# Mixing stage: homes of operands and order of the bonus changed; first stage: one norm chain for both token tiles

## The chip, the cores and the metric

The kernel runs on one core of one Trainium2 chip. The metric is device time in microseconds, as the median of several runs. Before the change it is 1272.42 us (three runs: 1272.36, 1272.42 and 1277.24).

## The reference

A decoder trunk of two layers on 256 tokens of width 1024, in float32. Each layer is

```python
x = x + 0.5 * swiglu_ffn(rms_norm(x, ffn1_norm_g[l]), ffn1_w_in[l], ffn1_w_out[l])
proj = rms_norm(x, mix_norm_g[l]) @ w_mix_in[l]
y_rwkv = rwkv7_time_mix(p_rwkv, ...)        # 8 heads of 64, state updated per token
y_moba = moba_attention(q_m, k_m, v_m, rel_bias)   # 8 heads, one causal block of 256
x = x + concat([y_rwkv, y_moba]) @ w_mix_out[l]
x = x + memory_cross_attention(rms_norm(x, xattn_norm_g[l]), rms_norm(mem, mem_norm_g[l]), w_q, w_kv, w_o)
x = x + 0.5 * swiglu_ffn(rms_norm(x, ffn2_norm_g[l]), ffn2_w_in[l], ffn2_w_out[l])
```

with a last RMS norm behind both layers. Within the time mix, `r`, `k` and `v` are columns of the projection, the state decays per token, and to its output comes the bonus `sum(r * k * r_k) * v` per head, before the gate g. The memory has 256 tokens, too; cross attention has 4 heads of 256.

## The kernel before, in words

*Precision and weights.* Every product runs as three TensorE matmuls: each operand is split into a rounded part `hi` and a remainder `lo`, and hi·hi, hi·lo and lo·hi are summed in PSUM (`mm3`). Weights arrive as 1 MB tiles `raw` that SyncE loads one after the other; two `raw` buffers exist, so a load is issued when the tile two before it has been split. A tile is split in two halves (or four quarters): ScalarE copies it to `whi`, VectorE subtracts to get `wlo` (`split`). Activations are split the same way: `xt` tiles hold hi and lo; ScalarE writes hi (copy, line 85), VectorE lo (lines 79 or 82).

*Stages.* A layer is: first feed-forward, mixing, cross attention, second feed-forward. In mixing (`rwkv`, `moba` and the generator `others`, which the stage's main loop interleaves) the time mix is computed in four chunks of 64 tokens, two chunks (`cp`) together. G is the accumulated decay and Gi its inverse; BK holds the chunk's b and k times Gi, ZL holds kk·G and r·G; their products are masked into XB and ZL, a triangular system is inverted (`both`, then M and W, assembled by VectorE from TensorE's transposes), and a sequential pass over the chunks gives y. The bonus lives in BV, which is the buffer of `km`: it is formed from r, k and r_k before r is multiplied by G, then multiplied by v, then gated. Between these steps TensorE works on the mixing's own projections (`in_w_mixa`), on the memory's K and V projections for cross attention (`in_w_k`, `in_w_v`, whose operand is `xt` from `memT`), and on MoBA's heads.

*Order.* Each engine runs its own list of instructions in a fixed order, which a scheduler makes from the order of the source and from hints (`after`, `marks`). Engines wait for one another through semaphores. A tile comes from a pool with a tag and a number of buffers (tag "e" 15 buffers, "xn" 4, each of the four tiles of an operand taking one); an operand in a tag can be written only when the former user of its buffer is done.

*Norms.* `norm_rows` sums squares of a token tile (ScalarE), adds them to v, and `rsqrt` finds the factor by an integer guess and Newton steps, seven small VectorE instructions on one column. In the first stage (`start`) this is done for two token tiles, one after the other; `spread` turns the two factors into a row rT, and two scaled copies `r` per tile serve ScalarE (`h`, line 352). Mixing's and cross attention's inputs are normed in `norm_T` (`xs`, line 208), transposed by TensorE (line 216) and split by `normed` into `xt`.

*Homes before.* The input operand xT of every stage has tag "xn", as has the memory's operand. For cross attention, K's transposed projection kT is evicted in mixing and split into an operand with tag "e" in `xattn`, under a hint that puts it into the MoBA stretch; so is Q's.

## Time and profile before

| what | value |
|---|---|
| median of three runs | 1272.42 us |
| profiled execution, time and span | 1276.54 us, 1274.5 us |
| granted TensorE clock | 0.998 of full speed |
| TensorE busy | 1255.0 us (98%), 8912 matmuls |
| TensorE weight loads busy | 1086.7 us (85%) |
| VectorE busy | 911.8 us (72%), 1713 instructions |
| ScalarE busy | 740.5 us (58%), 1385 instructions |
| DMA | 222.30 MB, mean 174 GB/s |

TensorE runs almost without a gap. In layer 0 mixing takes about 191 to 372 us of the span, cross attention until about 448, and layer 1 repeats layer 0 some 631 us later. A row of the timeline gives start, duration, engine, line, operation, output and inputs, shape and how many were merged; in brackets stands how long the engine idled ahead of it and who released it.

### The profile page before, as it was taken

To read this page: it belongs to the slowest core of one execution; us is meant where nothing else is said; L and a number is where in the kernel's file an instruction comes from. 1 tells how busy PE (TensorE), PEld (TensorE's weight loads), DVE (VectorE), ACT (ScalarE), POOL (GpSimd) and SP (SyncE) were. 2 spreads that over 40 slices of the span, in tenths; PEclk is the share of its full clock that TensorE was granted. 3 is DMA by queue.
4 is the path that set the end of the run, shared out by engine and by line. 5 is a ranking of instruction groups with operands and counts; after the bars stand their busy time and mean duration, and the time that the engine had idled before them with its cause. 6 is when DMAs were issued, how large, how long until landed. Compare 5 with 4: busy or idle time off the path is not lost.

```text
span 1274.5 us, 22364 instructions
## 1 busy us (share of the span) xinstructions
PE 1255.0 (98%) x8912; PEld 1086.7 (85%) x8912; DVE 911.8 (72%) x1713; ACT 740.5 (58%) x1385; POOL 50.0 (4%) x74
## 2 busy tenths in 40 slices
PE   9999999999999999999999999999999999999997
PEld 7888888998878888888888888899988798888886
DVE  7978557888787676665576665569888767766644
ACT  6755437675645565554365554467756545655543
POOL 0025000010000000000000000000100000000000
PEclk9999999999999999999999999999999999999999
DMA  8767653345244435555545546443441344445542
GB/s 296 262 227 264 223 220 133 131 145 174 85 165 167 158 133 176 195 186 211 198 146 185 198 173 232 174 164 135 166 151 39 132 178 165 166 175 188 196 171 96
DMA packets 36120, 222.30 MB, mean 174 GB/s; under 512 B 4616, under 2 KB 8240, under 8 KB 10800
## 3 DMA queue, kind: packets, MB, share of 16 engines
q1 hardware_dynamic: 33504, 213.06, 46.9%
q0 software_dynamic: 1936, 7.35, 1.8%
q8 instruction: 70, 1.15, 0.4%
q10 hardware_dynamic: 576, 0.46, 0.1%
q14 instruction: 34, 0.28, 0.1%
HBM read 218.75 MB, written 3.68 MB: 175 GB/s over the span
## 4 chain that ended last, share of the span: by engine, by line
PE 82%; DVE 9%; ACT 5%; DMA 2%; issue 2%; ACTq 0%; DVEq 0%; SPq 0%
PE acc L100 75%; PE pm L100 4%; DVE wlo L79 2%; ACT whi L85 1%; DMA raw<-in_w_q_dram 1%; PE tr L216 1%; PE tr L100 1%; DMA raw<-in_w_k_dram 1%; DVE km L82 1%; ACT e L451 0%; DVE wb L79 0%; DVE kk L79 0%; DVE BK L79 0%; DVE rt L82 0%; ACT UD L85 0%
## 5 line engine op out<-in xcount | busy, mean ns | idle before, releaser
L100 PE MATMUL acc<-xt,whi 128*128 128x512 f32 (+1 forms) x2496 | 679.9, 344 | 0.2
L79 DVE TENSOR_TENSOR wlo<-raw,whi 128x1024 fp32r<-128x1024 f32 (+1 forms) x450 | 461.1, 1040 | 237.8 <-ACT whi L85 236.6
L85 ACT ACTIVATE whi<-raw 128x1024 fp32r<-128x1024 f32 (+1 forms) x450 | 399.5, 910 | 338.0 <-PE acc L100 248.6
L100 PE MATMUL acc<-xt,wlo 128*128 128x256 f32 x1888 | 531.6, 282 | 0.8 <-DVE wlo L79 0.8
L100 PEld LDWEIGHTS acc<-xt,whi 128*128 128x128 f32 x2496 | 432.0, 190 | 64.2 <-issue 2.0
L100 PEld LDWEIGHTS acc<-xt,wlo 128*128 128x128 f32 x1888 | 358.8, 190 | 1.8 <-DVE wlo L79 1.1
L100 PE MATMUL acc<-whi,hT 128*128 128x512 f32 x704 | 218.5, 390 | 0.0
L100 PEld LDWEIGHTS acc<-whi,hT 128*128 128x128 f32 x704 | 132.2, 188 | 27.4
L100 PE MATMUL acc<-wlo,hT 128*128 128x512 f32 x352 | 137.2, 390 | 0.0
L100 PEld LDWEIGHTS acc<-wlo,hT 128*128 128x128 f32 x352 | 66.1, 188 | 13.8 <-DVE wlo L79 0.4
L79 DVE TENSOR_TENSOR z<-acc,z 128x256 f32<-128x256 f32 x160 | 66.9, 418 | 0.6 <-ACT z L85 0.3
L100 PE MATMUL acc<-wb,xt 128*128 128x512 f32 x240 | 62.6, 400 | 0.0
L85 ACT ACTIVATE z<-acc 128x256 f32<-128x256 f32 x160 | 58.7, 367 | 3.5 <-PE acc L100 3.3
L85 ACT ACTIVATE xt<-tr,par 128x128 fp32r<-128x128 f32 x112 | 37.8, 365 | 28.1 <-PE tr L216 17.7
L100 PEld LDWEIGHTS acc<-wb,xt 128*128 128x128 f32 x240 | 42.9, 188 | 9.9 <-ACT xt L85 1.9
L186 ACT ACTIVATE junk<-x 128x512 f32<-128x512 f32 x36 | 22.6, 629 | 44.6 <-DVE x L82 24.3
L82 DVE SCALAR_TENSOR_TENSOR xt<-tr,par,xt 128x128 fp32r<-128x128 f32 x112 | 35.9, 346 | 8.1 <-ACT xt L85 7.5
L100 PE MATMUL acc<-whi,oT 128*128 128x512 f32 x128 | 40.3, 394 | 0.0
L79 DVE TENSOR_TENSOR z<-z,z 128x256 f32<-128x256 f32 x80 | 34.0, 425 | 7.2
L85 ACT ACTIVATE hT<-z 128x256 fp32r<-128x256 f32 x80 | 32.0, 400 | 10.5 <-DVE z L79 10.5
L79 DVE TENSOR_TENSOR hT<-z,hT 128x256 fp32r<-128x256 f32 x80 | 33.5, 419 | 3.1 <-ACT hT L85 3.1
L373 ACT ACTIVATE z<-z 128x256 f32<-128x256 f32 x80 | 32.7, 409 | 0.3 <-DVE z L79 0.3
(271 smaller groups left out, 1189.7 us busy)
## 6 DMA issues: line engine op xcount, KB each, us to landing
raw<-in_w_f2i_dram SPq DMA_DIRECT2D x44, 1024.0 KB, 4.7
raw<-in_w_f1i_dram SPq DMA_DIRECT2D x42, 1024.0 KB, 4.8
raw<-in_w_f1o_dram SPq DMA_DIRECT2D x22, 1024.0 KB, 4.8
raw<-in_w_mixa_dram SPq DMA_DIRECT2D x22, 1024.0 KB, 4.8
raw<-in_w_f2o_dram SPq DMA_DIRECT2D x22, 1024.0 KB, 4.8
raw<-in_w_v_dram SPq DMA_DIRECT2D x8, 1024.0 KB, 4.8
raw<-in_w_k_dram SPq DMA_DIRECT2D x8, 1024.0 KB, 4.8
raw<-in_w_mixo_dram SPq DMA_DIRECT2D x8, 1024.0 KB, 4.9
```

The lines of the kernel that those rows point to most:

```text
L79: return V.tensor_tensor(out=out_, in0=a, in1=b, op=op)
L82: V.scalar_tensor_tensor(out_, a, s, b, op0=op0, op1=op1)
L85: return A.activation(out_, in_, AF.Copy, **k)
L100: return nc.tensor.matmul(o, a, b, start=start, stop=stop, skip_group_check=True).ins
L186: marks["square"] = A.activation(junk, xt[:, n * 512:(n + 1) * 512], AF.Square, scale=1.0 / 32.0, accum_out=ss[:, n:n + 1]).ins
L216: nc.tensor.transpose(p[:, k, :], xs[:, k * 128:(k + 1) * 128], ident)
L373: A.activation(sums[0], sums[0], AF.Silu)
```

## The change

Four edits. (1) `norm_rows` takes several token tiles and computes their factors as columns of one chain; the first stage and the memory's norm use it. (2) In mixing, r·G is written straight into ZL by VectorE; before, VectorE multiplied r by G in place and ScalarE copied it to ZL. The bonus's first step (km, from r) moves behind it. (3) The bonus's product with v moves behind the mark "half", which stands after the two additions to M. (4) Homes: cross attention's input xT moves from tag "xn" to "e", Q's operand from "e" to "xn"; the buffers for K's operand are taken at the end of mixing.

```diff
@@ -179,22 +179,28 @@
         V.tensor_scalar(aux[:, :, 8:12], par[:, :, P_LNG:P_LNG + 4], RS, None, op0=OP.mult)
 
 
-    def norm_rows(xt):
+    def square_sums(xt):
         ss = SM([128, 2], name="ss", tag="n2")
         for n in range(2):
             junk = SM([128, 512], name="junk", tag="k2")
             marks["square"] = A.activation(junk, xt[:, n * 512:(n + 1) * 512], AF.Square, scale=1.0 / 32.0,
                                            accum_out=ss[:, n:n + 1]).ins
-        v = SM([128, 1], name="v", tag="n1")
-        V.tensor_scalar(v, ss[:, 0:1], ss[:, 1:2], NORM_EPS, op0=OP.add, op1=OP.add)
-        return rsqrt(v, 1, "n1")
+        return ss
+
+    def norm_rows(*xs):
+
+        n = len(xs)
+        v = SM([128, n], name="v", tag="n1" if n == 1 else "n2")
+        for i, ss in enumerate([square_sums(z) for z in xs]):
+            V.tensor_scalar(v[:, i:i + 1], ss[:, 0:1], ss[:, 1:2], NORM_EPS, op0=OP.add, op1=OP.add)
+        return rsqrt(v, n, "n1" if n == 1 else "n2")
 
     def spread(rs):
 
         p = BANK("tr")
-        for t, r in enumerate(rs):
+        for t in range(2):
             rb = SM([128, 128], name="rb", tag="k1")
-            V.tensor_scalar(rb, r.to_broadcast([128, 128]), RS, None, op0=OP.mult)
+            V.tensor_scalar(rb, rs[:, t:t + 1].to_broadcast([128, 128]), RS, None, op0=OP.mult)
             nc.tensor.transpose(p[:, t * 128:(t + 1) * 128], rb, ident)
         rT = H([128, S], name="rT", tag="mo")
         copy(rT, p[:, 0:S])
@@ -231,14 +237,14 @@
     def put_pair(xT, j, src):
         split(xT[j][:, :, 0, :], xT[j][:, :, 1, :], src)
 
-    def normed(g):
+    def normed(g, tag):
 
         xT = []
 
         def do(t, later=False):
 
             if not xT:
-                xT.extend(XT())
+                xT.extend(XT(tag))
 
             def put(n, p):
                 for k in range(4):
@@ -396,7 +402,7 @@
                 elif i < 16:
                     nc.sync.dma_start(mems[n][:, j % 4, :], I["memt"][:, j, :])
             if i == 8:
-                rs = [norm_rows(z) for z in rows]
+                rs = norm_rows(*rows)
             elif i == 10:
                 rT = spread(rs)
             elif i > 10:
@@ -428,11 +434,11 @@
     def xattn(l, xT, kTf, vx, post, following):
 
         v, vgen = vx
-        kT = XT("e")
+        kTf, kT = kTf
         for j in range(4):
             with after([marks["chunk", 1]]):
                 put_pair(kT, j, kTf[j // 2][:, 2 * (j % 2):2 * (j % 2) + 2, :])
-        qT = XT("e")
+        qT = XT()
         oT = [None] * 4
         P_ = {}
 
@@ -700,19 +706,18 @@
         for cp in range(2):
             tt(BK[cp][:, :, :, 0:64], pv(a, cp), pv(Gi, cp), OP.mult)
             tt(BK[cp][:, :, :, 64:128], pv(km, cp), pv(Gi, cp), OP.mult)
-        BV = km
-        for p in range(4):
-            stt(BV[:, p, :], r[:, p, :], P(P_RK, p), km[:, p, :], OP.mult, OP.mult)
         ZL = [[None, None] for _ in range(2)]
         for cp in range(2):
             two = lambda z: ch(z)[:, :, 2 * cp:2 * cp + 2, :]
             tt(two(kk)[:, :, :, 1:64], two(kk)[:, :, :, 1:64], two(G)[:, :, :, 0:63], OP.mult)
-            tt(two(r), two(r), two(G), OP.mult)
             for e in range(2):
                 hs = half(e)
                 ZL[e][cp] = H([128, 2, 4, 128], name="ZL")
                 copy(ZL[e][cp][hs, :, :, uc(e)], pv(kk, cp)[hs])
-                copy(ZL[e][cp][hs, :, :, dc(e)], pv(r, cp)[hs])
+                tt(ZL[e][cp][hs, :, :, dc(e)], pv(r, cp)[hs], pv(G, cp)[hs], OP.mult)
+        BV = km
+        for p in range(4):
+            stt(BV[:, p, :], r[:, p, :], P(P_RK, p), km[:, p, :], OP.mult, OP.mult)
         shifted(6, v[:, 2:4])
         yield XA
         yield XBB
@@ -871,10 +876,11 @@
         spread_heads(bh, ph, C_TM)
         yield first
         values(1)
-        for n, z in enumerate(of_heads(bh, C_HT, "acc")):
-            tt(ch(BV)[:, :, n, :], z, ch(v)[:, :, n, :], OP.mult)
+        bonus = of_heads(bh, C_HT, "acc")
         yield next(levels)
         with after([marks["half"]]):
+            for n, z in enumerate(bonus):
+                tt(ch(BV)[:, :, n, :], z, ch(v)[:, :, n, :], OP.mult)
             for p in range(4):
                 stt(BV[:, p, :], BV[:, p, :], P(P_LNB, p), g[:, p, :], OP.add, OP.mult)
         yield from levels
@@ -1049,12 +1055,13 @@
                 while due > 0:
                     due -= next(fill, 1e9)
         run(fill)
+        kx = XT("e")
         run(og)
-        return kT, (v, lambda: run(v_block(mT, 1)))
+        return (kT, kx), (v, lambda: run(v_block(mT, 1)))
 
 
     norms = [(l, g) for l in range(L) for g in (G_FFN1, G_MIX, G_XA, G_FFN2)]
-    ops = [normed(par[:, l, g:g + 8]) for l, g in norms]
+    ops = [normed(par[:, l, g:g + 8], "e" if g == G_XA else "xn") for l, g in norms]
 
     def last(t, later=False):
         r = norm_rows(x[t])
@@ -1112,14 +1119,14 @@
             for i, j in ((0, 0), (1, 0), (0, 1)):
                 for t in range(2):
                     mm(acc[t], tok(xT0, k, t)[i], b[j], k == 0 and i + j == 0, k == KT - 1 and j == 1)
-        r = [norm_rows(x[t]) for t in range(2)]
+        r = norm_rows(*x)
+        scales = []
+        for f in (RS, 0.5 * RS):
+            z = SM([128, 2], name="r", tag="nr")
+            V.tensor_scalar(z, r, f, None, op0=OP.mult)
+            scales.append([z[:, t:t + 1] for t in range(2)])
         rT = spread(r)
-        rs, half_ = [], []
-        for t in range(2):
-            for z, f in ((rs, RS), (half_, 0.5 * RS)):
-                z.append(SM([128, 1], name="r", tag="nr"))
-                V.tensor_scalar(z[t], r[t], f, None, op0=OP.mult)
-        return acc, (rs, rT, half_)
+        return acc, (scales[0], rT, scales[1])
 
     first, scale = start()
     steps = memory()
```

VectorE's order in layer 0's mixing, before, from km to the first masks: wlo469 and wlo471 are the two halves of one in_w_mixa tile, raw467.

```order
L82 SCALAR_TENSOR_TENSOR km422_2426<-rkv382_2140,par_75,km422_2426 128x256 x4
L79 TENSOR_TENSOR wlo469_2783<-raw467_2780,whi468_2782 128x1024
L79 TENSOR_TENSOR rkv382_2140<-rkv382_2140,G409_2324 128x4x128 x2
L82 SCALAR_TENSOR_TENSOR rkv383_2141<-acc445_2605,par_75,rkv383_2141 128x255
L79 TENSOR_TENSOR wlo471_2785<-raw467_2780,whi470_2784 128x1024
L82 SCALAR_TENSOR_TENSOR rkv383_2141<-acc445_2605,par_75,rkv383_2141 128x255
L79 TENSOR_TENSOR XB457_2707<-pm462_2712,con_74 128x512
L79 TENSOR_TENSOR ZL441_2591<-pm463_2713,con_74 64x512
L79 TENSOR_TENSOR ZL442_2594<-pm463_2713,con_74 64x512
L79 TENSOR_TENSOR XB457_2707<-tr464_2730,con_74 128x512
L79 TENSOR_TENSOR ZL441_2591<-tr465_2731,con_74 64x512
L79 TENSOR_TENSOR ZL442_2594<-tr465_2731,con_74 64x512
```

After, behind the four new ZL products, from km on: wlo461 and wlo463 are the halves of that tile, raw459.

```order
L82 SCALAR_TENSOR_TENSOR km414_2408<-rkv374_2122,par_75,km414_2408 128x256 x4
L82 SCALAR_TENSOR_TENSOR rkv375_2123<-acc437_2585,par_75,rkv375_2123 128x255
L79 TENSOR_TENSOR wlo448_2658<-raw444_2653,whi447_2657 128x1024
L82 SCALAR_TENSOR_TENSOR rkv375_2123<-acc437_2585,par_75,rkv375_2123 128x255
L79 TENSOR_TENSOR wlo461_2763<-raw459_2760,whi460_2762 128x1024
L79 TENSOR_TENSOR XB449_2687<-pm454_2692,con_74 128x512
L79 TENSOR_TENSOR ZL433_2568<-pm455_2693,con_74 64x512
L79 TENSOR_TENSOR ZL434_2571<-pm455_2693,con_74 64x512
L79 TENSOR_TENSOR XB449_2687<-tr456_2710,con_74 128x512
L79 TENSOR_TENSOR ZL433_2568<-tr457_2711,con_74 64x512
L79 TENSOR_TENSOR ZL434_2571<-tr457_2711,con_74 64x512
L79 TENSOR_TENSOR wlo463_2765<-raw459_2760,whi462_2764 128x1024
```

The second half's subtract stood ahead of all six masks; it now stands behind them. The two products rkv<-rkv,G are gone from between.

VectorE's order at the transition from mixing to cross attention in layer 0, before: rs is the factor of the second token tile, xs its scaled rows, wlo733 the first part of the in_w_q tile.

```order
L82 SCALAR_TENSOR_TENSOR rs702_4388<-rt703_4389,rs702_4388 128x1
L208 TENSOR_SCALAR xs704_4396<-x1_73,rs702_4388 128x512
L208 TENSOR_SCALAR xs705_4397<-x1_73,rs702_4388 128x512
L82 SCALAR_TENSOR_TENSOR xt685_4307<-tr696_4329,par_75,xt685_4307 128x128
L79 TENSOR_TENSOR wlo733_4522<-raw731_4519,whi732_4521 128x512
L82 SCALAR_TENSOR_TENSOR xt685_4307<-tr696_4329,par_75,xt685_4307 128x128
L79 TENSOR_TENSOR wlo733_4522<-raw731_4519,whi732_4521 128x512
L79 TENSOR_TENSOR wlo735_4524<-raw731_4519,whi734_4523 128x512
L82 SCALAR_TENSOR_TENSOR xt684_4306<-tr706_4400,par_75,xt684_4306 128x128
```

After: wlo725 is the first part of the in_w_q tile, and the two xt<-kT shown are the last two of four subtracts of K's operand.

```order
L214 TENSOR_SCALAR xs700_4380<-x1_73,rs698_4372 128x512
L214 TENSOR_SCALAR xs701_4381<-x1_73,rs698_4372 128x512
L79 TENSOR_TENSOR xt668_4234<-kT510_3136,xt668_4234 128x2x256
L79 TENSOR_TENSOR xt669_4235<-kT510_3136,xt669_4235 128x2x256
L82 SCALAR_TENSOR_TENSOR xt680_4290<-tr702_4384,par_75,xt680_4290 128x128
L79 TENSOR_TENSOR v708_4422<-pm710_4424,v708_4422 128x512
L82 SCALAR_TENSOR_TENSOR xt682_4292<-tr703_4397,par_75,xt682_4292 128x128
L82 SCALAR_TENSOR_TENSOR xt680_4290<-tr702_4384,par_75,xt680_4290 128x128
L79 TENSOR_TENSOR v709_4423<-pm711_4425,v709_4423 128x512
L82 SCALAR_TENSOR_TENSOR xt681_4291<-tr702_4384,par_75,xt681_4291 128x128
L82 SCALAR_TENSOR_TENSOR xt682_4292<-tr703_4397,par_75,xt682_4292 128x128
L79 TENSOR_TENSOR wlo725_4502<-raw723_4499,whi724_4501 128x512
```

The subtracts of K's operand and the evictions of the second token tile now stand between xs and the first wlo of in_w_q; before, one eviction stood there.

## Rows read from the trace of the kernel before

**Rows 1.** The page, section 1: busy time, share of the span, instructions of each engine.
```profile
PE 1255.0 (98%) x8912; PEld 1086.7 (85%) x8912; DVE 911.8 (72%) x1713; ACT 740.5 (58%) x1385; POOL 50.0 (4%) x74
```
**Rows 2.** The page, section 4: the chain that ended last, by engine.
```profile
PE 82%; DVE 9%; ACT 5%; DMA 2%; issue 2%; ACTq 0%; DVEq 0%; SPq 0%
```
**Rows 3.** Waits of TensorE: us in total, times, longest.
```profile
PE tr L216 <- DVE xt L82: 2.8, 2, 1.6
PE tr L100 <- DVE W L79: 1.9, 2, 1.1
PE pm L100 <- ACT ZL L85: 1.3, 2, 0.7
```
**Rows 4.** Timeline of VectorE in the first stage: start, us, engine, line, operation.
```profile
18.02 0.21 DVE L189 TENSOR_SCALAR v<-ss 128x1 f32<-128x1 f32 x1
...
19.55 0.22 DVE L197 TENSOR_SCALAR rb<-rs 128x128 f32<-128x128 f32 x1
```
**Rows 5.** Timeline of ScalarE in the first stage.
```profile
18.93 0.19 ACT L186 ACTIVATION_READ_ACCUMULATOR junk<-x 128x1 f32 x1
19.99 0.47 ACT L352 ACTIVATE h<-acc,r 128x256 f32<-128x256 f32 x1 [0.88 <-DVE r L1121]
21.35 0.47 ACT L352 ACTIVATE h<-acc,r 128x256 f32<-128x256 f32 x1 [0.88 <-DVE r L1121]
```
**Rows 6.** Timeline of TensorE in the first stage.
```profile
24.62 0.39 PE L100 MATMUL acc<-xt,wlo 128*128 128x256 f32 x1 [0.77 <-DVE wlo L79]
```
**Rows 7.** Timelines of VectorE, ScalarE and TensorE around ZL, layer 0.
```profile
253.60 1.29 DVE L79 TENSOR_TENSOR rkv<-rkv,G 128x512 f32<-128x512 f32 x2
...
254.38 2.56 ACT L85 ACTIVATE ZL<-rkv 64x512 f32<-64x512 f32 x4 [2.04 <-DVE rkv L79]
...
255.70 0.99 PE L100 MATMUL pm<-ZL,BK 64*64 64x128 f32 x28 [0.65 <-ACT ZL L85]
```
**Rows 8.** Timeline of SyncE's DMA queue, 230 to 300; the duration spans the merged issues.
```profile
233.22 23.58 SPq L110 DMA_DIRECT2D raw<-in_w_mixa_dram  x4
264.29 3.51 SPq L110 DMA_DIRECT2D raw<-in_w_v_dram  x2
280.16 16.26 SPq L110 DMA_DIRECT2D raw<-in_w_k_dram  x4
```
**Rows 9.** DMA issues by tensor: count, KB each, median us from issue to landing.
```profile
raw<-in_w_mixa_dram SPq DMA_DIRECT2D x22, 1024.0 KB, 4.8
```
**Rows 10.** Timeline of VectorE, 261 to 312.
```profile
265.08 2.36 DVE L79 TENSOR_TENSOR wlo<-raw,whi 128x1024 fp32r<-128x1024 f32 x2 [0.82 <-ACT whi L85]
...
278.27 0.69 DVE L79 TENSOR_TENSOR xt<-memT,xt 128x512 fp32r<-128x512 f32 x1 [2.01 <-ACT xt L85]
...
302.32 1.23 DVE L79 TENSOR_TENSOR wlo<-raw,whi 128x1024 fp32r<-128x1024 f32 x1 [1.40 <-ACT whi L85]
```
**Rows 11.** Windows of 5 us: busy us (and instructions) of each engine, clock, DMA share, GB/s.
```profile
284.00:289.00 5.00, 5.00 (x24) 4.15 (x23) 4.72 (x14) 2.01 (x2) 0.00 (x0) 1.00 0.66 236
...
294.00:299.00 5.00, 5.00 (x129) 4.70 (x128) 5.00 (x9) 3.60 (x6) 0.00 (x0) 1.00 0.37 108
```
**Rows 12.** Timeline of TensorE at the inverse W, layer 0.
```profile
310.62 0.69 PE L100 MATMUL tr<-W,TB 32*32 32x32 f32 x32 [0.83 <-DVE W L79]
```
**Rows 13.** Timelines of VectorE and TensorE at the last half of y, layer 0.
```profile
361.77 1.29 DVE L79 TENSOR_TENSOR wlo<-raw,whi 128x512 fp32r<-128x512 f32 x2 [0.18 <-ACT whi L85]
...
365.12 0.17 DVE L79 TENSOR_TENSOR rt<-rs 128x8 f32<-128x8 f32 x1
...
367.86 0.66 PE L957 MATMUL tr<-con,y 128*128 128x128 f32 x4 [0.22 <-DVE y L79]
```
**Rows 14.** Timelines of SyncE's queue, ScalarE and TensorE at the transition to cross attention.
```profile
374.75 18.98 SPq L110 DMA_DIRECT2D raw<-in_w_q_dram  x4
...
381.66 1.67 ACT L85 ACTIVATE whi<-raw 128x512 fp32r<-128x512 f32 x3 [1.97 <-DMA raw<-in_w_q_dram]
...
384.88 0.66 PE L216 MATMUL tr<-con,xs 128*128 128x128 f32 x4 [1.63 <-DVE xt L82]
```

## The prediction

> **What bounds the kernel now.** I read the page first. TensorE is busy for 1255.0 of 1274.5 us and VectorE for 72% [rows 1], so the matmuls set the time and only the 20 us of TensorE's gaps can move. The chain of waits says the same: 82% of it is TensorE, 9% VectorE, 5% ScalarE [rows 2]. The list of TensorE's waits then names the gaps that touch the edited code: 2.8 us in the transposes that feed cross attention, behind VectorE's xt; 1.9 us at the inverse W, behind VectorE's W; 1.3 us at ZL, behind ScalarE's copies; each over both layers [rows 3]. After that I went through the timelines of VectorE, ScalarE and SyncE around these places. The changed program issues the same matmuls, so every term below is a gap that opens or closes. The sum is made against the profiled execution, 1276.5 us with its 1274.5 us span; that execution is 4.1 us above the median of the runs, 1272.4, and I add the sum to the median.
>
> **First stage.** Before, each token tile has a chain of its own: the first runs from v at 18.02 to rb at 19.55, 1.53 us for eight small instructions, 0.19 each [rows 4], and ScalarE scales the first h at 19.99, the second at 21.35 [rows 5]. After, one chain on two columns begins only when both sums of squares are there, at 19.12 (18.93 plus 0.19 [rows 5]). Eight VectorE instructions fall away here. An operation on 128x2 is not in the trace; 128x1 costs 0.19 in this chain and 128x8 took 0.17 [rows 4, 13], so I take 0.19 whatever the width. From 19.12, one v and eight steps give a factor at 20.85 and, with the two r, the first h at about 21.3 instead of 19.99; both rb are done at about 21.65, where the second one ended near 21.2 before (21.35 less its hand-over). Behind them on ScalarE stand rT, z and the next whi, about 0.35 later, and behind whi the wlo for which TensorE already waits 0.77 us [rows 6]. Ends: -0.8, if the eight saved instructions close that wait, and +1.3, if the whole delay of the first h reached it. I take +0.4, since it is the second h that stands directly before.
>
> The Trainium skill (Perfetto Trace Analysis, Optimizing Scalar/DVE Operations) says that grouping small operations can help an engine that is saturated, and that where VectorE is not saturated but causes gaps elsewhere, breaking instructions up may get the work done sooner. By the first half this edit gains, up to the 0.8 above; by the second it loses. The trace has TensorE waiting here with the first h done well ahead of the second [rows 5, 6], which sides with the second half; the sum with either stays inside the ends just given.
>
> **ZL, and what it pushes back.** Removed per layer: two products rkv<-rkv,G (1.29 us for both) and four ScalarE copies ZL<-rkv (2.56 us), for the last of which TensorE waits 0.65 us [rows 7]. The four copies from kk stay. Added: four VectorE products of 64x512, a form the trace lacks; nearest is the 128x512 product at 0.6 to 0.65 [rows 7], so 2.4 to 2.6 for the four. They stand right behind BK, ahead of km and of a wlo, and are done near 252.2 in the trace's frame, while TensorE arrives near 253.8 at the earliest. So its gap there goes: -0.8 per layer, the 0.65 and what its own sequencer adds.
>
> The price stands in VectorE's order above. Of the third mixa tile shown there, the second half's wlo (wlo471 before) stood ahead of the masks XB and ZL; its counterpart (wlo463) stands behind all six. A raw buffer is free again when its wlo are done, so SyncE's last mixa load moves. Before, it was out by 256.8 [rows 8]. Now that wlo ends at about 262.1 (the masks near 261, an estimate, plus 1.18 [rows 10]); at 4.8 us to landing [rows 9] the tile is there at 267, whereas VectorE began on its wlo at 265.08 before [rows 10]. These wlo in turn fall behind the masks of the second unit and end at about 272.4, in place of 267.4. On this the second in_w_v load waits: out by 267.8 before [rows 8], now 272.7. It lands at 277.4, its two whi are done at 279.3, and behind them ScalarE has the copies of the memory operand, so VectorE's subtract xt<-memT moves from 278.27 [rows 10] to about 279.9: +1.6 us.
>
> From there VectorE has no slack: it is busy for 4.72 of 5 us in 284 to 289 and for 5.00 of 5 in 294 to 299 [rows 11], so about 0.3 of the 1.6 is won back. The rest passes to the last of the four in_w_k loads (out by 296.4 [rows 8]), to the wlo that waits for its whi at 302.32 [rows 10], and through km and M to W, for which TensorE stops 0.83 us already [rows 12]. TensorE then stands 1.3 us later than before, the 0.8 of ZL spent. Ends per layer: -0.8, if the loads have slack that I don't see, and +4.9, the whole delay of the load. I take +1.2, near the delay of the subtract, because that is what the later chain hangs on.
>
> **Bonus behind the half mark.** Four km products move behind the two M additions, so M comes some 1.3 us earlier. W still stands behind the same products, the four scalings of km and one wlo, so its time is the same: 0, with one product of about 0.35 (half of a 128x512 one) either way.
>
> **kT splits.** Four copies on ScalarE and four subtracts of 128x512 on VectorE per layer leave the MoBA stretch. The subtract has the form of xt<-memT, 0.69 [rows 10], or 0.60 in a series. They make yl and y a little late there: -0.3 per layer, from 0 to -0.6, one subtract.
>
> The reordering also puts two wlo of the y group apart. Before, both at 361.77 filled the time in which ScalarE squares y, and TensorE waits 0.22 us for y at 367.86 [rows 13]. After, the reduction va comes first, VectorE idles for the square, and the wlo stand between va and rs. One wlo of 128x512 is 0.65 [rows 13]: +0.5 per layer, from 0 to +1.3, both.
>
> **The transition to cross attention.** Before, ScalarE sits until 381.66 on the first in_w_q tile, issued at 374.75, 6.9 us earlier; behind it stand the evictions of xt for which TensorE waits 1.63 us at 384.88 [rows 14]. After, cross attention's xT is in other buffers and most evictions of the first token tile stand ahead of that whi, so this wait goes: -1.6, in layer 1 -1.2 (2.8 less 1.6 [rows 3]). But the four kT splits now stand here, 4 x 0.60 = 2.4 us on VectorE. Two stand ahead of xs, so xs ends near 385.5, when TensorE arrives. The other two, and seven evictions and v subtracts of 0.3 to 0.6, stand ahead of the first wlo of in_w_q: 385.5, plus 1.2, plus 2.6, plus its own 0.65, is 389.95. TensorE, with no stop in front, reaches it near 387.65 and waits 2.3 us. With the stops of about 0.5 that this absorbs, net +0.4 per layer. Ends: -2.0, if the new wait doesn't come, and +2.4, if the splits add all of their time.
>
> **Sum.** Start +0.4; per layer +1.2 - 0.3 + 0.5 + 0.4 = +1.8; two layers +3.6; together +4.0 us. The feed-forward stages keep their work. The terms at W and at y lean on delays that the next idle stretch of VectorE may swallow, so I take 0.6 off: +3.4, 1272.4 + 3.4 = 1275.8 us.
>
> **Rivals.**
> (A) *The waits go and nothing takes their place.* Per layer -0.8 and -0.3, the transition -2.8 over both, the start +0.4: -4.6, and with the small stops behind the transposes -5.6: 1266.8 us. For it: each of these waits is the last link in its row. Against it: VectorE is nearly full in just the stretches into which work moves.
> (B) *Slower: the kT splits at the transition add up.* The place is the first wlo of in_w_q. If VectorE reaches xs later than I have it, 2.4 us of subtracts per layer come on top of the forecast: +3.4 + 4.8 = +8.2, 1280.6 us. It decides as soon as TensorE waits there for over 3.8 us per layer. For it: VectorE has the residual sum, the factor and the evictions to do at the same time. Against it: the first in_w_q load runs alone and lands earlier than 6.9 us after its issue.
> (C) *No change.* Gains and losses cancel, 98% of the span being TensorE: 1272.4 us, between 1270 and 1274.
>
> **Chances.** Forecast 0.40, A 0.20, B 0.18, C 0.22. About 0.5%, 6.4 us, is what a measurement of this kernel can tell from no change. Below 1266.1 lies under half of A and little else: 0.10. Above 1278.8 lies most of B and a tenth of the forecast: 0.20. Within: 0.70. The forecast's own range is 1273 to 1279; with most of A and half of B it becomes 1267 to 1280.5.
>
> **What would show it.** Right: the ZL wait is gone from TensorE's list; the last mixa load is out near 262.5 and the second in_w_v near 272.7; TensorE's wait at W is over 1.5 us in both layers; the wait for xt in the transposes is gone and one for the wlo of in_w_q, some 2 us, stands in its place; the wlo wait of the first stage is 1.1 to 1.2 us instead of 0.77. Wrong: the loads go out at the old times, the wait at W doesn't grow, or no wait above 1 us shows behind the kT splits; then it is A. A wait of 4 us there makes it B.

## The result and the profile after

The changed kernel takes 1278.9 us (median of 14 runs, 1276.8 to 1283.4), the kernel before, run beside it, 1272.4 (14 runs). The ratio is 1.0054, 95% interval 1.0042 to 1.0065: 6.9 us slower, where the prediction had 3.4. The profiled execution took 1279.2 us with a span of 1277.1; the profiled execution of before took 1276.5, which is 4.1 above its median, so differences between the two profiles are read stretch by stretch below.

The page, section 1 (busy time, share of the span, instructions) and section 4 (the chain that ended last), answer to [rows 1, 2]:

```profile
PE 1253.4 (98%) x8912; PEld 1087.0 (85%) x8912; DVE 912.5 (71%) x1707; ACT 734.8 (58%) x1377; POOL 55.8 (4%) x74
...
PE 80%; DVE 10%; ACT 5%; DMA 4%; issue 2%; ACTq 0%; DVEq 0%; SPq 0%
```

Same matmuls, six VectorE and eight ScalarE instructions fewer, and the chain leans more on VectorE and on DMA. ScalarE's busy time fell by 5.7 us, VectorE's did not fall (912.5 beside 911.8), and TensorE waits more. The list of TensorE's waits (us in total, times, longest) answers to [rows 3]:

```profile
PE acc L100 <- DVE wlo L79: 6.0, 4, 2.3
PE tr L100 <- DVE M L804: 2.4, 2, 1.2
PE tr L100 <- DVE W L79: 2.4, 2, 1.4
PE acc L100 <- ACT xt L85: 1.3, 2, 0.7
```

The waits for ZL and for xt in the transposes are gone. In their place stand two of 2.3 us for a wlo (the transition to cross attention), two of 1.2 us for M, which TensorE did not wait for here before, and a longer one for W. The last line is new, too: TensorE waits for xt, the memory's operand in the V projection, for which it did not wait before.

Next, the start: timelines of VectorE, ScalarE and TensorE in the first stage, as in [rows 4 to 6].

```profile
19.06 0.21 DVE L195 TENSOR_SCALAR v<-ss 128x1 f32<-128x1 f32 x1 [0.92 <-ACT junk L186]
...
20.89 0.24 DVE L1126 TENSOR_SCALAR r<-rs 128x2 f32<-128x2 f32 x2
...
21.15 0.84 ACT L358 ACTIVATE h<-acc,r 128x256 f32<-128x256 f32 x2 [2.12 <-DVE r L1126]
...
23.54 0.50 PE L100 MATMUL acc<-xt,whi 128*128 128x512 f32 x1 [0.38 <-ACT whi L85]
24.80 0.39 PE L100 MATMUL acc<-xt,wlo 128*128 128x256 f32 x1 [0.76 <-DVE wlo L79]
```

The joint chain begins at 19.06; both h run together from 21.15, and TensorE stops 0.38 us for whi, where it was 0.12 before, ahead of the old stop for wlo.

The same three engines and SyncE's queue around ZL in layer 0 answer to [rows 7, 8, 10, 12]. The frame is 0.8 us later than before's: TensorE's transposes of rh, ahead of all this, start at 239.46 here and at 238.67 before.

```profile
250.54 2.80 DVE L79 TENSOR_TENSOR ZL<-rkv,G 64x512 f32<-64x512 f32 x4
253.35 1.67 DVE L82 SCALAR_TENSOR_TENSOR km<-rkv,par,km 128x256 f32<-128x256 f32 x4
254.94 0.47 DVE L82 SCALAR_TENSOR_TENSOR rkv<-acc,par,rkv 128x255 f32<-128x255 f32 x1
255.34 1.22 DVE L79 TENSOR_TENSOR wlo<-raw,whi 128x1024 fp32r<-128x1024 f32 x1
...
262.05 1.21 DVE L79 TENSOR_TENSOR wlo<-raw,whi 128x1024 fp32r<-128x1024 f32 x1
...
281.14 0.69 DVE L79 TENSOR_TENSOR xt<-memT,xt 128x512 fp32r<-128x512 f32 x1 [4.33 <-ACT xt L85]
...
278.59 2.00 ACT L85 ACTIVATE whi<-raw 128x1024 fp32r<-128x1024 f32 x2 [2.46 <-DMA raw<-in_w_v_dram]
...
226.27 37.38 SPq L110 DMA_DIRECT2D raw<-in_w_mixa_dram  x5
267.23 6.62 SPq L110 DMA_DIRECT2D raw<-in_w_v_dram  x2
...
298.81 1.05 DVE L804 STREAM_TRANSPOSE M<-ex 128x512 f32<-128x512 f32 x1
...
300.00 0.74 PE L100 MATMUL tr<-M,UA 32*32 32x32 f32 x64 [1.21 <-DVE M L804]
```

TensorE no longer stops for ZL. The chain that the prediction wrote down is there with its times: the wlo behind the masks at 262.05, the last mixa load out by 263.65 (226.27 + 37.38), the second in_w_v by 273.85, xt<-memT at 281.14, which is 2.9 us later, or 2.1 in before's frame. But TensorE pays at xt itself (at most 0.7 us, by the list of waits) and then at M, some 13 us ahead of W, and one wlo stands late that the prediction had not looked at: the one at 255.34, which before ran at 249.74, right behind BK; in before's frame it is 4.8 us late.

At the transition (VectorE, TensorE and SyncE, as [rows 14]):

```profile
386.13 0.87 DVE L214 TENSOR_SCALAR xs<-x,rs 128x512 f32<-128x512 f32 x2
386.92 1.28 DVE L79 TENSOR_TENSOR xt<-kT,xt 128x512 fp32r<-128x512 f32 x2
...
390.92 0.68 DVE L79 TENSOR_TENSOR wlo<-raw,whi 128x512 fp32r<-128x512 f32 x1
...
391.66 0.39 PE L100 MATMUL acc<-xt,wlo 128*128 128x256 f32 x1 [2.27 <-DVE wlo L79]
...
376.89 20.19 SPq L110 DMA_DIRECT2D raw<-in_w_q_dram  x4
```

Two of the four kT splits stand ahead of xs, two behind, then seven evictions and v subtracts, then the wlo; TensorE waits 2.27 us for it.

To see where time goes, I measured the stretches between the starts of named transposes in TensorE's timeline, in every profile (rh, BK, M, W, rkv, y and the next feed-forward's input are the operands transposed, in order of time). They are differences of two rows each. For before they are, in layer 0: rh to BK 40.21, BK to M 18.50, M to W 13.24, W to rkv 21.26, rkv to y 35.98, y to the next feed-forward's input 79.98 (layer 1: 79.66). Differences to that, layer 0 / layer 1:

| kernel | rh–BK | BK–M | M–W | W–rkv | rkv–y | y–ffn2 |
|---|---|---|---|---|---|---|
| after | -0.7 / -0.7 | +2.6 / +2.4 | +0.1 / +0.1 | -0.2 / +1.3 | -1.0 / -1.0 | -0.5 / +0.9 |
| e1, start alone | 0 / 0 | 0 / 0 | -0.2 / -0.2 | 0 / 0 | 0 / 0 | -1.2 / -1.2 |
| e2, ZL alone | -0.7 / -0.7 | +2.5 / +2.4 | 0 / +0.4 | 0 / 0 | 0 / 0 | -1.6 / -1.0 |
| e3, bonus alone | 0 / 0 | 0 / 0 | 0 / 0 | -0.2 / -0.3 | 0 / 0 | -1.6 / -0.6 |
| e4, homes alone | 0 / 0 | 0 / 0 | -0.3 / -0.2 | 0 / 0 | -1.0 / -1.0 | -0.7 / -0.4 |
| e5, homes, kT late | 0 / 0 | 0 / 0 | -0.1 / -0.1 | 0 / 0 | -1.0 / -1.0 | -2.2 / -0.6 |
| e6, ZL for one pair | -0.7 / -0.7 | +2.0 / +1.7 | 0 / 0 | 0 / 0 | 0 / 0 | -1.6 / -0.7 |
| e10, ZL late | -0.7 / -0.7 | +0.9 / +1.9 | +0.3 / +0.4 | 0 / 0 | 0 / 0 | -1.6 / -1.1 |

The first three edits act in stretches ahead of y and the homes act from rkv on, so single edits can be read from after's trace. Differences of 0.3 in M–W stand in kernels whose edits don't touch it, and are no more than noise. The last column needs more care: e1 to e3 don't touch it and are yet 0.6 to 1.6 us shorter than before's profile. That profile had a late transition, to which I come back.

### The profile page after: what moved, and what is told of

Read it like the earlier page. It is cut to its first block, busy times and chain, and to the rows that moved or that the text cites. A ratio compares the mean times of both kernels' runs of the same rounds, so it can differ in the third digit from the quotient of the medians.

```text
span 1277.1 us, 22356 instructions
## 1 busy us (share of the span) xinstructions
PE 1253.4 (98%) x8912; PEld 1087.0 (85%) x8912; DVE 912.5 (71%) x1707; ACT 734.8 (58%) x1377; POOL 55.8 (4%) x74
## 4 chain that ended last, share of the span: by engine, by line
PE 80%; DVE 10%; ACT 5%; DMA 4%; issue 2%; ACTq 0%; DVEq 0%; SPq 0%
PE acc L100 73%; PE pm L100 4%; DVE wlo L79 3%; ACT whi L85 2%; DMA raw<-in_w_f1o_dram 1%; PE tr L222 1%; PE tr L100 1%; DMA raw<-in_w_f1i_dram 1%; DMA raw<-in_w_k_dram 1%; ACT xt L85 1%; DVE ZL L79 1%; ACT junk L186 0%; DMA raw<-in_w_f2i_dram 0%; DVE x L79 0%; DMA raw<-in_w_v_dram 0%
```

## Experiments

The times of all kernels that were run in several rounds:

| kernel | median, us | before beside it | ratio, 95% interval |
|---|---|---|---|
| e1_start | 1274.0 | 1272.1 | 1.0018, 1.0006 to 1.0029 |
| e2_zl | 1276.9 | 1272.1 | 1.0038, 1.0023 to 1.0053 |
| e3_bonus | 1270.2 | 1272.2 | 0.9989, 0.9976 to 1.0003 |
| e4_homes | 1273.2 | 1272.1 | 1.0012, 0.9999 to 1.0025 |
| e5_homes_kt_late | 1269.4 | 1272.1 | 0.9978, 0.9967 to 0.9989 |
| e6_zl_half | 1274.1 | 1272.2 | 1.0023, 1.0010 to 1.0036 |
| e8_after_kt_late | 1274.9 | 1272.2 | 1.0022, 1.0009 to 1.0035 |
| e9_best | 1271.3 | 1272.2 | 0.9997, 0.9982 to 1.0011 |
| e10_zl_late | 1274.1 | 1272.4 | 1.0012, 1.0000 to 1.0023 |
| e11_homes_bonus_late | 1269.2 | 1272.4 | 0.9978, 0.9965 to 0.9991 |
| e12_all_late | 1271.7 | 1272.4 | 0.9998, 0.9986 to 1.0011 |

**Each edit alone.** e1 is before plus edit 1, e2 plus edit 2, e3 plus edit 3, e4 plus edit 4 of the change; the core line of each:

```diff
+        r = norm_rows(*x)                                                       # e1
+                tt(ZL[e][cp][hs, :, :, dc(e)], pv(r, cp)[hs], pv(G, cp)[hs], OP.mult)   # e2
+            for n, z in enumerate(bonus):                  # e3, now behind marks["half"]
+    ops = [normed(par[:, l, g:g + 8], "e" if g == G_XA else "xn") for l, g in norms]    # e4
```

> The first stage's edit alone (one two-column norm chain), everything else as before. Theory (waits read from the traces): the chain starts only when both sums of squares are there, ScalarE's whi and the wlo behind it come 0.3 to 0.4 us later, and TensorE waits some 0.4 us more in all at 23 to 25 us: +0.4 us, 1272.8. Rival (the eight saved VectorE instructions let the wlo through earlier): the 0.77 us wait shrinks or goes, -0.8 us, 1271.6.

> The ZL edit alone (VectorE writes r*G into ZL, km behind it). Theory: the wait for ZL goes (-0.8 us per layer), but the wlo of the third mixa tile stands behind the six masks again, the last mixa load is out near 263 instead of 257 and the second in_w_v load near 273 instead of 268; TensorE then waits for xt from memT and longer at M and W: +1.7 us per layer, 1275.8; if TensorE's clock falls behind one of these waits, up to 1277.5. Rival (the loads have slack): only the ZL gap goes, -1.6 us, 1270.8.

> The bonus edit alone (its product with v behind the half mark). Theory: M comes earlier but W stands behind the same work, so nothing moves: 0 within 0.5 us. Rival (one product late, or a wlo moved with it, delays W): +0.6 us per layer, +1.2 in all. What the other three edits alone add up to (+8.6 us) against all four together (+6.8) would also leave room for a gain of up to 1.7 us here.

> The homes alone (cross attention's xT in e, its Q operand in xn, kT's buffers taken at the end of mixing). Theory from the two traces: TensorE's wait for xt in the transposes goes, a wait of 2.3 us for the first wlo of in_w_q comes in each layer, and small waits in MoBA and in cross attention go: -1.5 us per layer, -3 in all, 1269.4, less what half clock behind the 2.3 us wait takes back (1.7 us for each of two): between 1269 and 1273. Rival (the prediction's step): +0.6 us per layer, 1273.6.

By their ratios the four give +0.18, +0.38, -0.11 and +0.12%, together +0.57% beside the 0.54% of the whole: they add up within their intervals, and the ZL edit is the largest. ZL's time was as expected. The start came out above its expected 1272.8, and the homes lie just above their range of 1269 to 1273. The bonus's expected 0 lies inside its interval. In the traces, ZL nets -0.7 + 2.5 = +1.8 us in layer 0 and -0.7 + 2.4 + 0.4 = +2.1 in layer 1; the bonus -0.2 and -0.3. The homes give -1.0 at y in both layers (some 0.2 of it is one matmul of the yr group that now stands behind y's transposes and not ahead of them; they start every 0.23 us there), and then two waits of 2.3 us at the transition, as the list of waits of e4 shows (its third is the start's 0.8):

```profile
PE acc L100 <- DVE wlo L79: 5.3, 3, 2.3
```

The start gives +0.3 in e1's trace (TensorE's stops for whi and wlo are 0.43 + 0.77 us, before 0.12 + 0.77), but +2.3 (0.8 to 3.7) in the times. What makes up the rest is open.

**Are the kT splits the transition's cost?** e5 is e4 with each split moved into the score loop of its head, behind that head's q projection and without the hint; e8 is the changed kernel with the same move.

```diff
-        for j in range(4):
-            with after([marks["chunk", 1]]):
-                put_pair(kT, j, kTf[j // 2][:, 2 * (j % 2):2 * (j % 2) + 2, :])
...
             put_pair(qT, h, proj_a(xT, I["w_q"][l, h], CU["q"], () if h else [marks["scaled"]]))
+            put_pair(kT, h, kTf[h // 2][:, 2 * (h % 2):2 * (h % 2) + 2, :])
```

> The homes, but each quarter of kT is split only in the step that uses it, so that VectorE has the first wlo of in_w_q right behind xs. Theory (the four subtracts ahead of that wlo are what makes the 2.3 us wait): the wait falls below 0.5 us, no half clock there, -3 to -3.5 us per layer against before, 1265.5 to 1266.5. Rival (VectorE is full there whatever the order): another wait of about 2 us, for q or for the scores, takes its place and the time is that of the homes alone, 1269 to 1273.

> The changed kernel with one edit: each quarter of kT is split in the step that uses it. Theory: the 2.3 us wait for the wlo of in_w_q goes in both layers, and with it the half clock that followed it in some executions: -4 to -6 us against the changed kernel, 1273 to 1275; the cost of ZL stays. Rival (the waits are hidden by other waits later in cross attention): -2 us or less, 1277.

Yes. In both the 2.3 us waits are gone; e5 is 3.8 us below e4, e8 4.0 below the changed kernel, and e5 is faster than before. But e5's 1269.4 missed the 1265.5 to 1266.5 that I expected and lies in the rival's range. The layer-0 stretch from y is 77.73 us in e5, 1.5 below e4's; in layer 1 it is 79.03, only 0.2 below, with a wait of 1.21 us for pT. These 1.7 us are less than half of the 3.8; the rest goes with the granted clock of the other executions, as told under "Not foreseen". In e8 part of it comes back one stage later as a wait for pT (TensorE's list of waits of e8):

```profile
PE pm L100 <- ACT pT L85: 3.3, 2, 2.0
```

**Is it the wlo behind the masks?** That was the prediction's reason for ZL's loss. e6 makes the ZL edit for the first pair of chunks only (the bonus's first step is not moved), which puts that wlo ahead of the masks again; e9 is e5 with this half edit.

```diff
+            if cp:
+                tt(two(r), two(r), two(G), OP.mult)
...
+                if cp:
+                    copy(ZL[e][cp][hs, :, :, dc(e)], pv(r, cp)[hs])
+                else:
+                    tt(ZL[e][cp][hs, :, :, dc(e)], pv(r, cp)[hs], pv(G, cp)[hs], OP.mult)
```

> The ZL edit for the first pair of chunks only; the second pair keeps VectorE's product in place and ScalarE's copies. In VectorE's order both wlo of the third mixa tile stand ahead of the masks again, as before the change. Theory (the displaced wlo, not VectorE's four products, costs the time): the last mixa load is out near 257 again, the stretch from the BK transposes to M takes 18.5 us as before instead of 21.0, and the stretch ahead of it keeps the gain of 0.7: -0.7 us per layer, -1.4, against before. Rival (the products delay VectorE by themselves): the BK-to-M stretch still takes over 19.5 us and the time is that of before or above.

> Homes with kT split late, and the ZL edit for the first pair of chunks; the first stage and the bonus as before. Theory (the two repaired parts add): -2.8 of the first and -1.4 of the second, 1268. Rival (they share VectorE's slack): no better than the homes with kT split late, 1269.4.

No, or not alone: both expectations failed. BK to M stays at +2.0 in layer 0 and +1.7 in layer 1, e6 takes 0.23% more than before and not 1.4 us less, and e9 loses 1.9 us against e5. ScalarE's, VectorE's and TensorE's timelines of e6 show why:

```profile
259.55 1.06 ACT L85 ACTIVATE whi<-raw 128x1024 fp32r<-128x1024 f32 x1 [4.83 <-DMA raw<-in_w_mixa_dram]
...
253.16 2.35 DVE L79 TENSOR_TENSOR wlo<-raw,whi 128x1024 fp32r<-128x1024 f32 x2
...
298.06 0.74 PE L100 MATMUL tr<-M,UA 32*32 32x32 f32 x64 [1.19 <-DVE M L803]
```

Here too the wlo that stood between BK and km before (at 249.74) runs behind ZL and km, at 253.16. It ends the use of a raw buffer, so the fourth mixa load goes out late, and ScalarE stands 4.83 us before its whi.

**The other late wlo.** e10 makes the whole ZL edit but places the four products behind the first yield, so that the wlo behind BK keeps its place, while the other one stays behind the masks.

```diff
         yield XA
+        for cp in range(2):
+            for e in range(2):
+                hs = half(e)
+                tt(ZL[e][cp][hs, :, :, dc(e)], pv(r, cp)[hs], pv(G, cp)[hs], OP.mult)
         yield XBB
```

> Before plus the ZL edit alone, but with the four r.G products and the bonus's km placed behind the masks' first yield, so that the wlo that stood between BK and km (the second half of the mixa tile raw452) stands right behind BK again, ahead of the four products; the other wlo (wlo471) still stands behind the six masks. Theory 'the loss of the ZL edit comes from this first wlo, which frees the raw buffer 3.4 us late': the stretch from BK's first product to the transposes of M, 18.50 us before and 21.0 with the edit, falls to at most 19.3, the part ahead of it keeps its -0.7, the next mixa load's whi no longer waits 4.8 us, and the time is about 1271.5 to 1273. Rival 'it is the VectorE work itself (four 64x512 products) or the wlo behind the masks': the stretch stays at 20.2 to 21.0 and the time at 1274 to 1277.

The fourth and fifth mixa load of layer 0 in SyncE's queue, first before (of the five in [rows 8]), then after, e6 (two issues in one row) and e10:

```profile
251.03 0.33 SPq L110 DMA_DIRECT2D raw<-in_w_mixa_dram  x1
256.48 0.33 SPq L110 DMA_DIRECT2D raw<-in_w_mixa_dram  x1
```
```profile
256.62 0.33 SPq L110 DMA_DIRECT2D raw<-in_w_mixa_dram  x1
263.32 0.33 SPq L110 DMA_DIRECT2D raw<-in_w_mixa_dram  x1
```
```profile
254.44 2.99 SPq L110 DMA_DIRECT2D raw<-in_w_mixa_dram  x2
```
```profile
250.86 0.33 SPq L110 DMA_DIRECT2D raw<-in_w_mixa_dram  x1
262.37 0.33 SPq L110 DMA_DIRECT2D raw<-in_w_mixa_dram  x1
```

So e6 delays only the fourth load much, e10 only the fifth, after both. In layer 0, from rh to W, e6 costs +1.3 us and e10 +0.5 (-0.7 + 0.9 + 0.3), together the +1.8 of e2; in layer 1 +1.0 and +1.6 beside +2.1. Neither theory of mine held alone: each late wlo holds back a load and each costs. The expectation for e10, at most 19.3 us, failed narrowly in layer 0 (19.45) and clearly in layer 1 (20.43). A version with the ZL edit and neither wlo late was not run.

The rival in e10's expectation, VectorE's own work, can be read from the traces kept. The four products take 2.80 us and the two that fell away took 1.29 [rows 7], so VectorE has 1.5 us more to do. But it stands idle for 4.33 us ahead of xt<-memT at 281.14, where it stood 2.01 before [rows 10], and behind that subtract nothing has changed: M's write follows it by 17.67 us before (295.94 - 278.27) and after (298.81 - 281.14), and by 17.66 to 17.70 in both layers of e2, e6 and e10. So M is as late as xt<-memT is, and xt<-memT waits for ScalarE; VectorE's added work can count only through the loads that its wlo release.

**Combinations.** e11 is e5 with the bonus edit, e12 is e11 with e10's ZL; neither has the start edit.

> Before plus the homes with the kT splits in the score loop right behind each q projection, and the bonus behind the half mark; without the start and ZL edits. If single edits add up (-3.0 and -2.1 us as timed apart) 1267 to 1268 us, the fastest; the trace shows -0.2 per layer between W and rkv, -1.0 to y, about -2 and -0.6 to the px of cross attention. Rival: the two share the same slack of VectorE before y, then 1269 to 1270, as with the homes alone.

> Before plus homes with late kT splits, bonus, and the ZL edit in its late place; only the start edit is missing. If the first wlo is the cause of ZL's loss, -0.7 per layer comes on top of the kernel without the ZL edit: about 1266 to 1267. If not, +2 per layer: 1271 to 1272.

e11 equals e5, as its rival had it: the bonus adds nothing that can be measured. The ZL edit costs 2.5 us even in its late place, the second case of e12's expectation. The two best kernels, e5 and e11, are 0.2% faster than before; no version with the ZL edit beats the same one without.

**What a wait does to the clock.** e13 is before with repeats of one VectorE subtract (same values) at four places of each feed-forward's first product, so that TensorE must wait there.

```diff
+    more = [3, 4, 5, 6, 4, 5, 6, 7, 3, 4, 5, 6, 4, 5, 6, 7]
...
+            for half_ in unit(w_in[j], CU["ffn"], extra=more.pop(0) if j in (6, 10, 14, 18) else 0):
```

> Before, with 3 to 7 repeats of one VectorE subtract (wlo, same values) put in at four places of each feed-forward's first product, sixteen in all, so that TensorE must wait for wlo there, for times from about 1 to 8 us. If a wait of more than about 1.4 us is followed by a stretch of half granted clock by the length of the wait, all waits above a length show one and those below none. If it is by chance, long and short waits show it alike, in part of the places. The time itself is 20 to 60 us above before.

In its one execution, which took 1315.1 us, seven stops of 2.1 us or more came of it (2.10, 2.11, 2.84, 3.57, 4.71 twice, and 2.25 followed at once by 2.07), one of 1.84 and one of 0.91. TensorE's timeline at two of them, and windows behind them (us; then busy time of PE, PEld, DVE, ACT, POOL; granted clock; DMA share; GB/s):

```profile
550.57 0.58 PE L100 MATMUL acc<-xt,wlo 128*128 128x256 f32 x1 [2.10 <-DVE wlo L79]
...
746.45 0.39 PE L100 MATMUL acc<-xt,wlo 128*128 128x256 f32 x1 [1.84 <-DVE wlo L79]
```
```profile
551.00:553.00 2.00, 2.00 (x8) 1.71 (x8) 2.00 (x2) 0.00 (x0) 0.00 (x0) 0.50 0.00 0
...
746.50:750.50 4.00, 4.00 (x24) 3.54 (x25) 3.59 (x6) 1.12 (x3) 0.00 (x0) 1.00 0.78 260
```

Behind every one of the seven, and behind neither of the shorter two, the granted clock is 0.50 for some 3 to 6 us. That sides with the wait's length. But the other profiles have exceptions both ways, as told at the end.

## Why the prediction was right or wrong

**The whole.** Slower, inside the range, by twice the forecast. That the changed kernel would lose small amounts in several places, with ZL's reordering as the largest, was right. That the sum came so near is in part luck: ZL cost more than its term, y and the removed wait were mis-sized in opposite directions, and about as much as the whole forecast came from half clock, which it did not contain.

**Start, +0.4: near right in the trace.** One v and eight steps from 19.06 gave r at 20.89 and h at 21.15, as worked out (19.12, 20.85, 21.3). TensorE's stops are 0.38 + 0.76 = 1.14 us, within the 1.1 to 1.2 forecast, but the stop for whi was 0.12 before, which the prediction left out: +0.25, in e1 +0.3. Nor do eight VectorE instructions fall away here, but six: the chain behind v has six steps on one column and eight on two. The memory's norm saves four more, and e1 has 1703 in all beside 1713. The Trainium skill (Perfetto Trace Analysis, Optimizing Scalar/DVE Operations) says that where VectorE is not saturated but opens gaps elsewhere, breaking instructions up may let the work be done sooner; here six instructions fewer came with 0.3 us more of waiting, which agrees.

**ZL, +1.2 per layer: +2.0 and +1.8 came; the chain was right, but a second late wlo and the size were not.** The gain came as forecast (-0.7 for -0.8), though the four products took 2.80 us where 2.4 to 2.6 were put. In before's frame (0.8 less than the rows) the last mixa load is out by 262.9 and the second in_w_v by 273.1, where 262.5 and 272.7 were forecast; xt<-memT comes at 280.35, +2.1 us where +1.6 was forecast. Two steps failed. "About 0.3 of the 1.6 is won back": nothing was, as the 17.67 us above show. And the four products stand "ahead of km and of a wlo", where that wlo was costed at nothing. It frees a raw buffer, and its delay of 4.8 us in before's frame (255.34 against 249.74) went in full to the fourth mixa load (256.62 against 251.03). In e10, where it keeps its place, ZL costs 0.5 and 1.6 us and not 1.8 and 2.1. And the place of payment was M, not W. In before's timelines of VectorE and TensorE M has hardly any slack:

```profile
295.94 1.08 DVE L799 STREAM_TRANSPOSE M<-ex 128x512 f32<-128x512 f32 x1
...
297.38 0.75 PE L100 MATMUL tr<-M,UA 32*32 32x32 f32 x64
```

M is written by 297.02 and TensorE starts on it at 297.38 without a stop, so a wait that is in no list stood next in line. W's waits, 0.97 and 1.45 us, stayed under the 1.5 that I had named; that sign of being right did not come.

**Bonus, 0: right.** It is -0.2 per layer in the stretch behind W, and not to be told from 0 in the times. The wait at W in layer 1 is 1.39 us in e3, but the stretch from M to W is as before.

**MoBA and y, +0.2 per layer: wrong, about -0.8.** The reordering that I costed at +0.5 is there: va at 363.50, two wlo behind it, then rs. But TensorE's wait for y did not grow, it went (after's timelines of VectorE and TensorE):

```profile
368.64 0.69 DVE L79 TENSOR_TENSOR y<-y,rs 128x512 f32<-128x512 f32 x1
...
369.38 0.66 PE L963 MATMUL tr<-con,y 128*128 128x128 f32 x4
```

VectorE ends y at 369.33 and TensorE starts on it at 369.38. The homes edit gave more here than the one subtract that I had set as the bound: -1.0 from rkv to y, less the 0.2 of the matmul that only changed its place. No run separates the four splits that left from the reordering.

**Transition, +0.4 per layer: the new wait right to the tenth, the removed one not.** The wlo wait was forecast at 2.3 and is 2.27. But the 1.63 and 1.16 us that I took off (as 1.6 and 1.2) belong to one execution, and to one that I had noted as 4.1 us above the median. In before's profile the first in_w_q tile is issued at 374.75 and ScalarE starts on it at 381.66, 6.9 us later [rows 14]. ScalarE and TensorE in e1's timeline, where the issue is at 374.99:

```profile
380.68 1.68 ACT L85 ACTIVATE whi<-raw 128x512 fp32r<-128x512 f32 x3 [0.77 <-DMA raw<-in_w_q_dram]
...
383.91 0.66 PE L222 MATMUL tr<-con,xs 128*128 128x128 f32 x4 [0.43 <-DVE xt L82]
```

5.7 us, and the wait is 0.43 in layer 0 and none in layer 1; e2's profile has none in layer 0 and 0.16 in layer 1, e3's none and 0.61. So most of that gain was not there to be had. Something else made up for it, which I had not counted: between the transition and the next feed-forward, e1's TensorE loses some 2 us in small gaps of 0.1 to 0.4 us around pT and the scores in layer 0 (starts that come later than the form's usual pace), and e4's under 1. Against e1, from rkv to the next feed-forward's input, the homes in e4 are worth -0.5 us in layer 0 (-1.0 - 0.7 + 1.2) and -0.3 in layer 1, where the prediction's three steps add up to +0.6.

**Not foreseen: the clock.** In layer 1 two of after's waits are followed by half clock (below). It costs 1.5 us behind W (+1.3 in the table, where the bonus alone has -0.2 to -0.3) and 1.3 behind the transition (+0.9 against e4's -0.4), in that profile. It is not that execution alone. The record has the mean granted clock of every execution: on average 0.9960 over the 14 of the changed kernel and 0.9985 over the 31 of before that ran beside e1. Of a span of 1277 us the difference is some 3 us; as an estimate from these figures, that much of the 6.9 is half clock. Of the single edits it comes mostly with the homes (e4's executions have 0.9971), a little with the bonus (e3's 0.9981) and not with ZL (e2's 0.9986). It also closes the account of the kT splits: from e4 to e5 (0.9987) the clock is worth some 2.0 us, which with the 1.7 of the stretches makes 3.7 of the measured 3.8.

**Sum.** Against e1's undelayed transition, after's trace has: start +0.3, ZL +3.8 (2.0 and 1.8 from rh to W), bonus -0.4, homes -0.5 (layer 0 -1.0 - 0.5 + 1.2; layer 1 -1.0 + 0.9 + 1.2, less the 1.3), half clock +2.8: +6.0, near the measured 6.9. The 0.6 that I had shaved off for idle stretches was shaved the wrong way. Rival B's 1280.6 was near, but not its reason: no wait of 4 us stands behind the splits.

## What to carry to other kernels

When a step is moved, follow every subtract that it moves past to the buffer it frees and the load that waits for it, not just the ones whose place catches the eye; and look for links that have no wait now only because they arrive with no slack. Before crediting the removal of a wait that a DMA ends, check against another execution, or the other layer, whether it is always there; a profiled execution well above the median is a reason to doubt its waits. A wait on the matmul engine can cost more than its length, if the clock falls behind it; the granted clock of every execution shows how often it does.

## What the hardware showed

*Half clock behind a wait.* Windows of the changed kernel in layer 1, around the wait for W at 943.03 and behind the one for wlo at 1022.82 (TensorE's timeline, then windows with columns as above):

```profile
943.03 0.69 PE L100 MATMUL tr<-W,TB 32*32 32x32 f32 x32 [1.45 <-DVE W L79]
...
943.00:944.00 1.00, 0.97 (x34) 0.96 (x35) 0.95 (x3) 0.24 (x1) 0.00 (x0) 0.99 0.00 0
944.00:947.00 3.00, 3.00 (x17) 3.00 (x16) 2.56 (x14) 2.37 (x10) 0.72 (x1) 0.50 0.17 30
...
1022.00:1025.00 3.00, 2.18 (x10) 2.18 (x11) 3.00 (x8) 1.36 (x4) 0.00 (x0) 0.58 0.00 0
```

TensorE stood for 1.45 us, worked for 1 us at full clock, and then had 0.50 of it (the lower of the two levels, 1.2 of 2.4 GHz) for some 3 us although it was busy throughout; a group of three matmuls started every 0.64 us instead of every 0.36. The same 2.27 us wait in layer 0 and both of e4 had no such stretch, nor had waits at W of 1.37 and 1.39 us in e8 and e3 or one of 2.00 for pT in e8, while those at W of 1.36 in e11 and 1.45 in e12 and one of 1.69 for pT in e12 had one. In these profiles length alone doesn't decide up to 2.28 us; in e13 every wait from 2.1 on was followed by it. What decides between is open.

*Two speeds of the same matmul.* The feed-forward's 128x512 matmuls of layer 1, busy us and mean ns by form, first before, then after, window 680 to 780:

```profile
L100 PE MATMUL acc<-xt,whi 128*128 128x512 f32 x235 | 83.1, 399 | 0.0
```
```profile
L100 PE MATMUL acc<-xt,whi 128*128 128x512 f32 x237 | 82.2, 391 | 0.0
```

399 or 391 ns in a whole pass at a granted clock of 1.00; a pair with its 128x256 matmul starts every 353.3 or 346.7 ns, over 315 pairs 2.1 us. Of the three passes behind the first, before's profile has the slower in all, e9's the faster in all, after's the faster in one; no edit touches them. That is why stretches were compared here, and not whole profiles.
